# Stick-breaking attention: running sums over a softplus split in a high and a low part

## The chip, the cores and the metric

The kernel runs on one core of one Trainium2 chip. The metric is the device time of one execution in microseconds (us). Three runs of the kernel before took 1545.80, 1546.03 and 1546.11 us, the median is 1546.03 us. One more execution was profiled; its trace is what the rows below are from.

## The reference

One layer of a hybrid decoder, for 256 tokens of width 2048. The normalised input is projected (`h @ w_in`) into three parallel branches of width 1024 and their gates: a gated MLP over chunks of 128 tokens, a complex diagonal state space model (S5) followed by a GLU, and a stick-breaking attention of 8 heads. The branches are projected back, gated, summed, sent through `w_out`, and a squared-ReLU MLP of width 8192 and a last norm follow. All of it is float32.

The change lies in the attention. For each head and block of 128 queries:

```
z = q @ k.T * scale                          # 128 queries x up to 256 keys
log_1m = where(mask, log_sigmoid(-z), 0)     # minus the softplus of z
after  = cumsum(log_1m, reverse) - log_1m    # sum over the keys behind this one
w = where(mask, exp(log_sigmoid(z) + after), 0)
out = w @ v
```

The exclusive reverse running sum `after` is computed as a product with a strictly triangular matrix of minus ones, and, for keys in the other block, a matrix of minus ones.

## The kernel before, in words

**The main stream.** Every large product is cut into *units* of one 512 KB weight tile. For each unit SyncE loads the float32 tile (line 195), ScalarE casts it to fp32r (`hi`, line 214) and VectorE forms the rest `raw - hi` (`lo`, line 215, shown in the trace as L86, the helper through which all VectorE work is issued). TensorE then multiplies three combinations of high and low parts of weight and activation. `begin_unit` (line 260) converts the unit three ahead, so TensorE has two to three units in hand. There are four `hi` and four `lo` buffers: the cast of unit u+4 waits until TensorE is through with the `hi` of unit u. The units stand in a fixed plan (lines 154 to 185): S5 input, q, k, v for heads 0 to 3, then q, k, v for heads 4 to 7, the gated MLP, eight gates and branches, the four gates of the S5 branch (`gate1`), the GLU (`glu`), the rest. A unit is eight products of one weight part and four or eight more; it takes TensorE about 2.7 to 2.8 us.

**The side tasks.** Attention, S5 and the small preparations are Python generators. After every unit `pump` (line 224) goes through the list of tasks and issues steps of them. The order on each engine is the order in which the program is written; only GpSimd's is left to the scheduler. What `pump` issues after unit n stands on TensorE between the units n and n+1, and on ScalarE and VectorE behind the conversion issued with unit n.

**The account of `pump`.** VectorE's calls are metered in planner's nanoseconds, `(180 if n <= 128 else 65) + n * (0.52 if fast else 1.042)` for n elements per partition (line 85; `tensor_scalar` is fast, `tensor_sub` is not). After each unit the credit rises by 2560 and falls by what was metered since, with a cap of 5120; in short:

```
credit[0] = min(credit[0] + UNIT_NS - V.spent, NCRED * UNIT_NS)
V.spent = 0.0
for ent in list(tasks):
    while credit[0] > V.spent:
        c = next(ent[1])          # one step of the task
        if c == BAR: break        # go on with it after the next unit
```

A task that yields `BAR` stops until the next pump; a yielded number is compared with `BAR` and used for nothing else. Attention is put at the front of the list, `s5` at its end. `drain(name)` (line 237) runs a task to its end at once, with no unit between its steps; `do_glu` (line 1069) calls `drain("s5")`, since the GLU needs S5's output `gs`.

**S5's end** (lines 793 to 832): 16 chunks, each ending in a rotation of four VectorE steps (`rotate`); then `BAR`, `BAR`, the product `y_mm(7)` on TensorE (line 772), `BAR`, `y_evac(7)` (one VectorE operation and a Gelu on ScalarE, lines 778 and 780), `BAR`, and four `split2` (line 399), each a cast on ScalarE and a subtraction on VectorE, which give `gs`.

**Attention** (line 838): four pairs of heads. For a pair: scores `pz` (lines 847, 848), `BAR`, scaled copy and mask `za`, `BAR`, Abs, Exp and Ln on ScalarE (lines 861 to 863), `BAR` twice, then two VectorE operations of 768 elements that give the softplus `sp` and, in place, `za` (lines 866, 867), `BAR`, the running sums `pc` (lines 873 to 876), `BAR`, `le = pc + za` and Exp (lines 880 to 882), `BAR`, the product with v, `pyc` (lines 890, 892), `BAR`, the split of the output. The three blocks of `sp` lie side by side in a row of 384 columns: (keys 0, queries 0), (keys 0, queries 1), (keys 1, queries 1). All operands of `pc` are float32. The tiles of activations come from one pool of 32 buffers (`a4`, line 130).

Of the kernel before, what the change touches and what calls it, by code (L numbers as in the profile page):

```python
# [10 lines left out]
F32 = mybir.dt.float32  # L11
F32R = mybir.dt.float32r
I32 = mybir.dt.int32
AF = mybir.ActivationFunctionType
ALU = mybir.AluOpType
AX = mybir.AxisListType

P = 128
D = 2048
T = 256  # L20
# [71 lines left out]
def hybrid_trunk(  # L92
# [22 lines left out]
    V, S, G, PE = Metered(nc.vector), nc.scalar, nc.gpsimd, nc.tensor  # L115
# [14 lines left out]
    def a4(shape, dt, name):  # L130
        return acts.tile(shape, dt, tag="a4", name=name)
# [3 lines left out]
    def cst(shape, name, dt=F32):  # L135
        return const.tile(shape, dt, tag=name, name=name)

    def t2k(shape, name):
        return s5w.tile(shape, F32, tag="t2k", name=name)

    def side(name):
        return ps_sd.tile([P, 512], F32, tag="sd", name=name)
# [250 lines left out]
    def split1(dst, kt, src):  # L393
        S.copy(dst.hi(kt), src)
        V.tensor_sub(dst.lo(kt), src, dst.hi(kt).bitcast(F32))
# [35 lines left out]
    def load_x(c):  # L431
# [19 lines left out]
    ones = cst([P, P], "ones")  # L451
# [1 line left out]
    ident = cst([P, P], "ident")  # L453
    G.affine_select(out=ident, in_=ones, pattern=[[1, P]], compare_op=ALU.is_equal,
                    fill=0.0, base=0, channel_multiplier=-1)
    nones = cst([P, P], "nones")
    G.memset(nones, -1.0)

    ntri = cst([P, P], "ntri")
    G.affine_select(out=ntri, in_=nones, pattern=[[-1, P]], compare_op=ALU.is_gt,  # L460
                    fill=0.0, base=0, channel_multiplier=1)


    pw = side("pwarm")
# [373 lines left out]
    def attention(half):  # L838
        scale = 1.0 / math.sqrt(P)
        fl = "p e b t -> p (e b t)"  # L840
        for hb in (2 * half, 2 * half + 1):
            hs = (2 * hb, 2 * hb + 1)
            pz = []
            for h in hs:
                q, k = qT[h // 4][:, h % 4, :], kT[h // 4][:, h % 4, :]
                p = side(f"pz{h}")
                PE.matmul(p[:, 0:T], lhsT=k[:, 0:P], rhs=q, start=True, stop=True)
                PE.matmul(p[:, T:T + P], lhsT=k[:, P:T], rhs=q[:, P:T], start=True, stop=True)
                pz.append(p)
            yield BAR  # L850
            za = a4([P, 2, 3, P], F32, f"za{hb}")
            le = a4([P, 2, 3, P], F32, f"le{hb}")
            for e in range(2):
                S.activation(za[:, e].rearrange("p b t -> p (b t)"), pz[e][:, 0:T + P], AF.Copy, scale=scale)

                G.affine_select(out=za[:, e, 0:3:2, :], in_=za[:, e, 0:3:2, :], pattern=[[0, 2], [1, P]],
                                compare_op=ALU.is_gt, fill=-1e30, base=0, channel_multiplier=-1)
            yield BAR
            sp = a4([P, 2, 3, P], F32, f"sp{hb}")
            zf, lf, sf = za.rearrange(fl), le.rearrange(fl), sp.rearrange(fl)  # L860
            S.activation(lf, zf, AF.Abs)
            S.activation(lf, lf, AF.Exp, scale=-1.0)
            S.activation(lf, lf, AF.Ln, bias=1.0)
            yield BAR
            yield BAR
            V.scalar_tensor_tensor(out=sf, in0=zf, scalar=0.0, in1=lf, op0=ALU.max, op1=ALU.add)
            V.scalar_tensor_tensor(out=zf, in0=zf, scalar=0.0, in1=lf, op0=ALU.min, op1=ALU.subtract)
            yield 1700
            yield BAR
            pcs = []  # L870
            for e, h in enumerate(hs):
                pc = side(f"pc{h}")
                PE.matmul(pc[:, 0:T], lhsT=ntri, rhs=sp[:, e, 0:2, :].rearrange("p b t -> p (b t)"),
                          start=True, stop=False)
                PE.matmul(pc[:, P:T], lhsT=nones, rhs=sp[:, e, 2, :], start=False, stop=True)
                PE.matmul(pc[:, T:T + P], lhsT=ntri, rhs=sp[:, e, 2, :], start=True, stop=True)
                pcs.append(pc)
            yield BAR
            for e in range(2):
                V.tensor_add(le[:, e].rearrange("p b t -> p (b t)"), pcs[e][:, 0:T + P],  # L880
                             za[:, e].rearrange("p b t -> p (b t)"))
            S.activation(lf, lf, AF.Exp)
            yield 1000
            yield BAR
            v = vN[hb // 2]
            pys = []
            for e, h in enumerate(hs):
                p = side(f"pyc{h}")
                c0 = (h % 4) * P
                PE.matmul(p[:, 0:T], lhsT=v[:, 0, c0:c0 + P],  # L890
                          rhs=le[:, e, 0:2, :].rearrange("p b t -> p (b t)"), start=True, stop=False)
                PE.matmul(p[:, P:T], lhsT=v[:, 1, c0:c0 + P], rhs=le[:, e, 2, :], start=False, stop=True)
                pys.append(p)
            yield BAR
            for e, h in enumerate(hs):
                split1(yc, h, pys[e][:, 0:T])
            yield 700
# [105 lines left out]
    def do_nat(kind, i, us):  # L1003
        dsts = vN if kind == "v" else vg

        def ev(tt, ps):
            if tt == 0:
                dsts[i] = a4([P, NT, 512], F32, f"{kind}{i}")
            dst = dsts[i]
            S.activation(dst[:, tt, :], ps, AF.Gelu_apprx_tanh if kind == "vg" else AF.Copy,  # L1010
                         scale=r1[0][:, tt:tt + 1])
            if kind == "vg":
                sumsq(dst[:, tt, :], ssv[:, tt, i:i + 1], ps)
            if kind == "v" and tt == 1:
                spawn(f"att{i}", attention(i))
            if kind == "vg" and i == 1 and tt == 1:
                spawn("gmlp", gmlp())

        if kind == "vg" and i == 1:
            gmlp_load()  # L1020
        run_N(us, xs, ev)
# [253 lines left out]
```

## Time and profile before

| what | value |
|---|---|
| median of three runs | 1546.03 us |
| profiled execution | 1545.78 us, its span 1544.1 us |
| TensorE busy | 1528.4 us (99%) |
| VectorE busy | 1097.1 us (71%) |
| ScalarE busy | 764.0 us (49%) |
| mean granted TensorE clock | 0.998 |

The span runs from the first to the last instruction of the profiled execution. A line such as `L873 PE MATMUL pc<-sp,ntri` names the line of the kernel, the engine (PE is TensorE, PEld its weight load, DVE VectorE, ACT ScalarE, POOL GpSimd), the operation, and the tiles written and read. A float32 product appears as two pairs of weight load and matmul, an fp32r product as one. The durations of matmuls include their fill and drain, so that neighbours overlap; what a product costs in a stream is the distance of the starts.

### The profile page before, as it was taken

How to read it: one execution, taken by the hardware profiler on the slowest of the kernel's cores; microseconds unless marked ns; L12 is line 12 of the kernel's file. 1: busy time of each engine (PE TensorE's matmuls, PEld its weight loads, DVE VectorE, ACT ScalarE, POOL GpSimd, SP SyncE). 2: the span in 40 equal slices, each digit the busy share in tenths (PEclk: the TensorE clock that was granted, in tenths of full speed). 3: DMA queues.
4: the chain of work that ended last, by engine and by line, in shares of the span. 5: the costliest groups of instructions: out<-in, count | busy, mean ns of one | idle time of the engine just before them, and what ended most of it. 6: DMA issues, size and time to landing. Idle time of an engine off the chain costs nothing.

```text
span 1544.1 us, 20755 instructions
## 1 busy us (share of the span) xinstructions
PE 1528.4 (99%) x7900; PEld 1303.8 (84%) x7900; DVE 1097.1 (71%) x1454; ACT 764.0 (49%) x947; POOL 67.3 (4%) x126
## 2 busy tenths in 40 slices
PE   9999999999999999999999999999999999999997
PEld 9988888888888888898888888888888888888886
DVE  6886988989999999967655665466545564556554
ACT  7546577555546555564444443344434444344442
POOL 0301021001001000000000000000000000000000
PEclk9999999999999999999999999999999999999999
DMA  9965565657666666656666555555555555555653
GB/s 342 328 199 164 186 211 172 197 175 225 202 212 212 199 215 200 192 177 209 205 202 194 188 189 193 196 187 188 192 195 191 188 188 193 195 190 187 219 194 105
DMA packets 97411, 308.67 MB, mean 200 GB/s; under 512 B 11296, under 2 KB 22560, under 8 KB 97312
## 3 DMA queue, kind: packets, MB, share of 16 engines
q1 hardware_dynamic: 79200, 285.25, 56.2%
q0 software_dynamic: 11904, 10.49, 3.2%
q10 hardware_dynamic: 6208, 11.61, 2.4%
q8 instruction: 62, 1.02, 0.3%
q14 instruction: 37, 0.30, 0.1%
HBM read 301.02 MB, written 6.29 MB: 199 GB/s over the span
## 4 chain that ended last, share of the span: by engine, by line
PE 96%; DVE 1%; issue 1%; ACT 1%; DMA 1%; SPq 0%; POOLq 0%; POOL 0%; DVEq 0%; ACTq 0%
PE mm L289 21%; PE mm L351 19%; PE mm L352 19%; PE mm L354 19%; PE mm L293 11%; PE mm L320 1%; PE mm L321 1%; PE mm L328 1%; PE py L772 1%; PE pb L674 0%; DMA raw<-in_w_in 0%; ACT hi L214 0%; DVE lo L86 0%; DMA raw<-in_w_m 0%; DVE x L86 0%
## 5 line engine op out<-in xcount | busy, mean ns | idle before, releaser
L86 DVE TENSOR_TENSOR lo<-raw,hi 128x1024 fp32r<-128x1024 f32 (+1 forms) x537 | 653.3, 1220 | 380.1 <-ACT hi L214 365.5
L214 ACT CAST hi<-raw 128x1024 fp32r<-128x1024 f32 (+1 forms) x537 | 561.4, 1049 | 634.7 <-PE mm L352 397.7
L289 PE MATMUL mm<-xz,hi 128*128 128x512 f32 x1024 | 256.5, 392 | 0.0
L289 PEld LDWEIGHTS mm<-xz,hi 128*128 128x128 f32 x1024 | 184.4, 189 | 33.2
L351 PE MATMUL mm<-hi,xs 128*128 128x512 f32 x512 | 200.8, 392 | 0.0
L352 PE MATMUL mm<-hi,xs 128*128 128x512 f32 x512 | 199.5, 390 | 0.0
L352 PE MATMUL mm<-hi,ff 128*128 128x512 f32 x480 | 186.8, 389 | 0.0
L351 PE MATMUL mm<-hi,ff 128*128 128x512 f32 x480 | 186.8, 389 | 0.0
L293 PEld LDWEIGHTS mm<-xz,lo 128*128 128x128 f32 x1024 | 139.7, 190 | 10.0
L293 PE MATMUL mm<-xz,lo 128*128 128x256 f32 x1024 | 142.8, 282 | 0.0
L354 PE MATMUL mm<-lo,xs 128*128 128x512 f32 x512 | 137.0, 389 | 0.0
L354 PE MATMUL mm<-lo,ff 128*128 128x512 f32 x480 | 128.3, 389 | 0.0
L351 PEld LDWEIGHTS mm<-hi,xs 128*128 128x128 f32 x512 | 96.1, 188 | 21.9 <-ACT bu L681 1.6
L354 PEld LDWEIGHTS mm<-lo,xs 128*128 128x128 f32 x512 | 96.1, 188 | 20.2
L352 PEld LDWEIGHTS mm<-hi,xs 128*128 128x128 f32 x512 | 96.2, 188 | 19.4
L352 PEld LDWEIGHTS mm<-hi,ff 128*128 128x128 f32 x480 | 90.1, 188 | 18.7
L354 PEld LDWEIGHTS mm<-lo,ff 128*128 128x128 f32 x480 | 90.1, 188 | 18.7
L351 PEld LDWEIGHTS mm<-hi,ff 128*128 128x128 f32 x480 | 90.1, 188 | 18.6
L289 PE MATMUL mm<-xs,hi 128*128 128x512 f32 x384 | 96.6, 393 | 0.3 <-DVE s5x L86 0.3
L289 PEld LDWEIGHTS mm<-xs,hi 128*128 128x128 f32 x384 | 69.1, 189 | 13.3 <-ACT hi L214 0.5
L86 DVE TENSOR_TENSOR rt<-bu,cs 128x1024 f32<-128x1024 f32 x64 | 76.8, 1221 | 0.3
L293 PEld LDWEIGHTS mm<-xs,lo 128*128 128x128 f32 x384 | 52.4, 190 | 3.8
(252 smaller groups left out, 1681.3 us busy)
## 6 DMA issues: line engine op xcount, KB each, us to landing
raw<-in_w_m SPq DMA_DIRECT2D x256, 512.0 KB, 4.3
raw<-in_w_in SPq DMA_DIRECT2D x143, 512.0 KB, 4.2
raw<-in_w_wide SPq DMA_DIRECT2D x48, 512.0 KB, 4.4
raw<-in_w_br SPq DMA_DIRECT2D x48, 512.0 KB, 4.3
raw<-in_w_out SPq DMA_DIRECT2D x32, 512.0 KB, 3.8
x<-in_x ACTq DMA_DIRECT2D x8, 512.0 KB, 5.8
raw<-in_w_glu SPq DMA_DIRECT2D x8, 512.0 KB, 4.3
bs<-bd POOLq DMA_DIRECT2D x48, 64.0 KB, 4.7
```

The source lines that it names most:

```text
L86: return fn(*a, **kw)
L214: S.copy(hi[:, k, :], raw[:, k, :])
L289: PE.matmul(pt[:, nb, :], lhsT=hi[:, k, nb * P:(nb + 1) * P], rhs=src.both(4 * i + k), start=4 * i + k == 0, stop=False)
L293: PE.matmul(pt[:, nb, T:], lhsT=lo[:, k, nb * P:(nb + 1) * P], rhs=src.hi(4 * i + k), start=False, stop=4 * i + k == last)
L320: PE.matmul(po, lhsT=wh, rhs=src.hi(kt), start=kt == 0 and nb % 2 == 0, stop=False)
L321: PE.matmul(po, lhsT=wh, rhs=src.lo(kt), start=False, stop=False)
L328: PE.matmul(po, lhsT=lo[:, k, nb * P:(nb + 1) * P], rhs=src.hi(kt), start=False, stop=kt == 2 * nk - 1 and nb % 2 == 1)
L351: PE.matmul(ps[tt], lhsT=xh, rhs=hi[:, k, :], start=kt == 0, stop=False)
L352: PE.matmul(ps[tt], lhsT=xl, rhs=hi[:, k, :], start=False, stop=False)
L354: PE.matmul(ps[tt], lhsT=xh, rhs=lo[:, k, :], start=False, stop=kt == 2 * nk - 1)
L772: PE.matmul(py[h][32 * i:32 * i + 32, :T], lhsT=cks[h][:, ri, i, :], rhs=s[i // 2][:, ri, i % 2, :], start=ri == 0, stop=ri == 1, tile_pos ...
```

## The change

`sp` is split after it is computed: `sh` is its fp32r cast (ScalarE), `sl` the rest (VectorE). The running sums are then fp32r products: for `sh` and for `sl` one of 384 columns with the triangular matrix, over all three blocks at once, and one of 128 columns with the matrix of minus ones. Both constant matrices become fp32r, written by VectorE (`tensor_scalar`) in place of GpSimd; the triangular one is first built by GpSimd in a tile `tri` of the two-buffer pool `t2k`. The number yielded behind the step changes.

```diff
-    nones = cst([P, P], "nones")
-    G.memset(nones, -1.0)
-
-    ntri = cst([P, P], "ntri")
-    G.affine_select(out=ntri, in_=nones, pattern=[[-1, P]], compare_op=ALU.is_gt,
+    nones = cst([P, P], "nones", F32R)
+    V.tensor_scalar(out=nones, in0=ones, scalar1=-1.0, scalar2=None, op0=ALU.mult)
+
+    ntri = cst([P, P], "ntri", F32R)
+    tri = t2k([P, P], "tri")
+    G.affine_select(out=tri, in_=ones, pattern=[[-1, P]], compare_op=ALU.is_gt,
                     fill=0.0, base=0, channel_multiplier=1)
+    V.tensor_scalar(out=ntri, in0=tri, scalar1=-1.0, scalar2=None, op0=ALU.mult)
...
             V.scalar_tensor_tensor(out=zf, in0=zf, scalar=0.0, in1=lf, op0=ALU.min, op1=ALU.subtract)
-            yield 1700
+            sh, sl = (a4([P, 2, 3, P], F32R, f"sp{n}{hb}") for n in "hl")
+            S.copy(sh, sp)
+            V.tensor_sub(sl, sp, sh.bitcast(F32))
+            yield 2600
             yield BAR
             pcs = []
             for e, h in enumerate(hs):
                 pc = side(f"pc{h}")
-                PE.matmul(pc[:, 0:T], lhsT=ntri, rhs=sp[:, e, 0:2, :].rearrange("p b t -> p (b t)"),
-                          start=True, stop=False)
-                PE.matmul(pc[:, P:T], lhsT=nones, rhs=sp[:, e, 2, :], start=False, stop=True)
-                PE.matmul(pc[:, T:T + P], lhsT=ntri, rhs=sp[:, e, 2, :], start=True, stop=True)
+                for n, s in enumerate((sh, sl)):
+                    PE.matmul(pc[:, 0:T + P], lhsT=ntri, rhs=s[:, e].rearrange("p b t -> p (b t)"),
+                              start=n == 0, stop=False)
+                    PE.matmul(pc[:, P:T], lhsT=nones, rhs=s[:, e, 2, :], start=False, stop=n == 1)
                 pcs.append(pc)
```

## Rows read from the trace of the kernel before

**Rows 1.** The page, busy time of each engine and its share of the span.

```profile
PE 1528.4 (99%) x7900; PEld 1303.8 (84%) x7900; DVE 1097.1 (71%) x1454; ACT 764.0 (49%) x947; POOL 67.3 (4%) x126
```

**Rows 2.** Timeline of TensorE around the second pair's sums: start us, duration us, what.

```profile
171.57 2.00 PE L289 MATMUL mm<-xs,hi 128*128 128x512 f32 x8
173.41 1.12 PE L293 MATMUL mm<-xs,lo 128*128 128x256 f32 x8
174.37 0.60 PE L873 MATMUL pc<-sp,ntri 128*128 128x256 f32 x2
...
176.36 0.39 PE L352 MATMUL mm<-hi,xs 128*128 128x512 f32 x1
```

**Rows 3.** Timeline of the opening, GpSimd, TensorE and VectorE.

```profile
1.05 4.84 PE L467 MATMUL pwarm<-ones 128*128 128x128 f32 x24 [1.05 <-POOL ones L452]
...
1.44 0.28 POOL L460 TENSOR_SCALAR_AFFINE_SELECT ntri<-nones 128x128 f32<-128x128 f32 x1
...
4.27 0.89 DVE L86 SCALAR_TENSOR_TENSOR xs<-xf,colv,xs 128x256 fp32r<-128x256 f32 x2 [3.18 <-ACT xs L419]
```

**Rows 4.** Timeline of the first pair's softplus and sums, on three engines.

```profile
128.14 0.84 ACT L861 ACTIVATE le<-za 128x768 f32<-128x768 f32 x1
...
133.20 1.03 ACT L214 CAST hi<-raw 128x1024 fp32r<-128x1024 f32 x1
...
134.27 1.23 DVE L86 TENSOR_TENSOR lo<-raw,hi 128x1024 fp32r<-128x1024 f32 x1 [4.77 <-ACT hi L214]
...
135.09 0.58 ACT L302 COPY wq<-mm 128x512 f32<-128x512 f32 x1
...
137.66 1.28 ACT L732 ACTIVATE td<-cs,s_cs 128x128 f32<-128x128 f32 x4 [1.99 <-DVE cs L86]
...
138.16 1.11 PE L293 MATMUL mm<-xs,lo 128*128 128x256 f32 x8
...
140.00 0.95 DVE L86 SCALAR_TENSOR_TENSOR sp<-za,le 128x768 f32<-128x768 f32 x1
140.99 0.96 DVE L86 SCALAR_TENSOR_TENSOR za<-za,le 128x768 f32<-128x768 f32 x1
...
141.01 0.70 PE L873 MATMUL pc<-sp,ntri 128*128 128x256 f32 x2 [1.73 <-DVE sp L86]
...
142.76 0.55 PEld L674 LDWEIGHTS pb<-su,bs 96*128 96x128 f32 x4
...
143.00 1.13 DVE L86 SCALAR_TENSOR_TENSOR cs<-cs,s_cs,td 128x128 f32<-128x128 f32 x4
```

**Rows 5.** Timeline, the exponential behind the sums, first pair and second pair.

```profile
145.19 1.01 DVE L86 TENSOR_TENSOR le<-pc,za 128x384 f32<-128x384 f32 x2
...
146.28 1.28 ACT L882 ACT_TABLE_LOAD   x1 [5.45 <-DVE le L86]
...
182.50 0.85 ACT L882 ACTIVATE le<-le 128x768 f32<-128x768 f32 x1 [1.97 <-DVE le L86]
```

**Rows 6.** Timeline of S5's end and the first unit of the GLU.

```profile
655.00 1.28 DVE L86 TENSOR_TENSOR bu<-rt,rt 128x512 f32<-128x512 f32 x2
656.21 3.72 DVE L86 TENSOR_TENSOR lo<-raw,hi 128x1024 fp32r<-128x1024 f32 x3
...
661.13 1.07 PE L772 MATMUL py<-bu,ck 128*32 128x256 f32 x16
...
662.56 0.47 DVE L86 SCALAR_TENSOR_TENSOR s5x<-s5x,colv,py 128x256 f32<-128x256 f32 x1
...
664.03 2.50 DVE L86 TENSOR_TENSOR gs<-s5x,gs 128x512 fp32r<-128x512 f32 x4 [0.99 <-ACT gs L400]
...
665.03 0.28 PE L320 MATMUL mm<-gs,hi 128*128 128x256 f32 x1
```

**Rows 7.** Stretches near the end: stretch, us, busy of PE, PEld, DVE, ACT, POOL, PEclk, DMA.

```profile
1532.00:1533.00 1.00, 0.80 (x7) 0.59 (x5) 0.16 (x1) 0.00 (x0) 0.00 (x0) 1.00 0.00 0
...
1537.00:1538.00 1.00, 0.00 (x0) 0.00 (x0) 0.00 (x0) 0.00 (x0) 0.00 (x0) 0.82 1.10 324
```

## The prediction, made before the kernel was run

> **What bounds the kernel now.** I read the page first: TensorE is busy for 1528.4 of 1544.1 us, so 15.7 us are idle, nearly all of it in the opening and behind the last product; VectorE and ScalarE have 71% and 49% [rows 1]. The list of waits then gives TensorE one real wait in the middle, and it is at this very line: 1.73 us for the first pair's softplus [rows 4]. Last I read the timeline at that wait, at a pair that does not wait, and at the place where S5's result is handed to the GLU. TensorE time removed is therefore time won, but only where VectorE and ScalarE still deliver in time; and the side tasks are rationed by pump's account, so VectorE work added anywhere pushes S5's end back.
>
> **The running sums, pairs two to four.** In the second pair two heads' sums begin at 174.37; the second product behind them starts at 176.36, 0.23 after the first, so 1.76 us for two heads, 0.88 for one [rows 2]. An fp32r product of 512 columns costs (173.41 - 171.57) / 8 = 0.23, one of 256 columns (174.37 - 173.41) / 8 = 0.12 [rows 2]; 384 columns lie between, 0.17. An fp32r product of 128 columns has no row. Its ends: half of a 256-column one, 0.06; or as many passes as float32, 512 column steps, 0.22. I take 0.12, the nearest row, since each such product still loads 128 columns of weights. A head then costs 2 x (0.17 + 0.12) = 0.58 and wins 0.30: six heads, **-1.8 us** (ends -2.5 and -0.6). Each of these pairs gains units between softplus and sums, so the added cast and subtraction are covered: followed through the code, pump's account puts the sums 4, 3 and 4 pumps behind the softplus, where it was 2. Without that cover each pair would wait up to 1.8 us.
>
> **Startup.** VectorE now makes both constants. It waits for GpSimd's last select, done at 1.72, and has nothing else from its memsets to 4.27, after 3.18 us idle [rows 3]. Time: none; uncovered, two operations of half the columns of the pair that takes 0.89 there, so 0.5 at most. But the planner charges them 2 x (180 + 128 x 0.52) = 493.
>
> **Pair one.** When v is done (unit 40) the account stands at 191; less 493 it is negative, so attention starts one unit later. Sums still follow the softplus by one pump. A unit of q is 8 x 0.23 + 8 x 0.12 = 2.8 [rows 2]; unit 45 ends at 138.16 + 1.11 = 139.27, unit 46 at 142.07. ScalarE's Abs, Exp and Ln take 128.14 to 133.20, 5.1 us [rows 4]; one unit later they run from 130.9 to 136.0, and the next hi (1.03) is there at 137.05. VectorE, idle for it, then has the same work ahead of the softplus as it had from 134.27 to 140.00: two lo, the q evacuation, an S5 table, 5.73 us [rows 4]. The softplus starts at 142.8 and is done (0.95) at 143.7. The cast `sh` lies between a copy of 512 columns, 0.58, and a cast of 1024, 1.03 [rows 4]: 0.82, done at 144.6. `za` ends at 144.65; the subtraction, at `sp`'s 0.95, at 145.55. TensorE stands still from 142.07 to 144.65, does one head's high part, waits for `sl`, and has 0.29 + 0.58 left: done at 146.45. From the unit's end that is 4.4 us; before it was 142.76 - 139.27 = 3.5 [rows 4]. **+0.9 us** (ends: no wait left, -2.3; one more lo of 1.22 ahead of the softplus, +2.1).
>
> **What is late next.** ScalarE now does the S5 copies `td` (1.28) behind `sh`, so the next hi is there at 146.9; VectorE waits for it, does that lo, the table (1.13) and another lo [rows 4], and reaches `le` at 150.5, done at 151.5 [rows 5]. Exp needs 0.85, and 1.28 more if the table is loaded only after the wait, as in pair one; in pair two it did not come between [rows 5]. It is ready at 152.3 or 153.6; TensorE asks for it after the S5 product (0.55) and two units, at 152.6. Wait 0 or 1.0: **+0.5 us**. The main stream behind does not wait: it is three units ahead.
>
> **S5's end.** The planner is charged 4 x (65 + 768 x 1.042) = 3461 for the four subtractions, with startup 3954. Until here the account's highest value is 4475 of 5120, so none of it is forgiven. Attention goes first; S5 pays. A unit with no other VectorE work leaves 2560 - (65 + 1024 x 1.042) = 1428, so S5 comes 2.8 units later. Does it have them? The last rotation ends, three units' lo follow with no task between, `y_mm(7)` stands at 661.13, one unit comes behind it, and the GLU starts at 665.03 [rows 6]. Call that last unit L. Before, the rotation ends in the pump of L-4 (account 916, charged 1197), the two BARs take L-3 and L-2, `y_mm` comes in L-1, `y_evac` in L, the splits in the drain. At L-2 the account would be 2575, less 3954 it is -1379, more than the last two steps (1197): not done. At L-1 it is 4003 - 3954 = 49: just done. L takes the second BAR, and the drain issues `y_mm`, `y_evac` and splits with no unit between. TensorE then waits out the chain that the last unit hid: VectorE's 0.47 at once, Gelu, cast, first subtraction (a quarter of 2.50): 662.56 to 664.03 + 0.63, 2.1 us [rows 6]. **+2.1 us** (ends: 0, if `y_mm` still stands ahead of L; 3.3, if a lo of 1.2 sits before it on VectorE).
>
> **The rest.** The yielded 2600 is read by nobody. ScalarE gains 4 x 0.82, VectorE 4 x 0.95; behind them wait the next hi and lo, which are three units early. Eight more tiles in the pool of 32: no row shows a wait that they would add; between 0 and 1 us, I take 0. SP's queue is not touched, GpSimd loses a memset.
>
> **Sum:** -1.8 + 0.9 + 0.5 + 2.1 = +1.7. The profiled execution took 1545.78, its span 1544.1; it lies 0.25 below the median of 1546.03, so 1547.5 there and **1547.7** against the median. A measurement of this kernel can tell about 0.2%, 3.1 us, from no change: this is inside.
>
> **The rivals.**
> (a) *TensorE-bound throughout*, both waits absent: -1.8 - 2.3 = -4.1, 1541.9. For it: 99% busy. Against it: both places have no unit to spare by the code's own order. 0.05.
> (b) *S5 still in time*, if the account is other than I follow: +1.7 - 2.1 = -0.4, 1545.6. The margin of 49 only decides how late, not whether. 0.10.
> (c) *Cheap narrow products*, at 0.06: -2.5 + 0.7 + 0.5 + 2.1 = +0.8, 1546.8. For it: half the columns of a 256 one; against it: the weights are no fewer. The Trainium skill ("TensorE: Matmul & The Clock Gate", Back-to-back issue gap) puts a pair of load and 128-column product at about 81 ns, which would be an estimate of +1.1; no row here shows it. 0.12.
> (d) *Narrow products are as slow as float32*, in `pc`'s products with `nones`, 0.22 each: -0.6 + 1.2 + 0.5 + 2.1 = +3.2, 1549.2, **slower**. It decides from 0.21 on. For it: no fp32r product under 256 columns is in the trace; against it: nothing in the rows shows cost rising as columns fall. 0.12.
> (e) *The clock falls* in pair one's wait of 2.6 us. The rows: full clock through the 1.73 us wait; behind the last product (1532.8) it fell only within 1537 to 1538 [rows 7]. Price: the opening's 24 products took 4.84 us, 0.20 each where full clock needs 0.11 (a 256-column pass is as long), 2.2 us [rows 2, 3]: +3.9, 1549.9. The Trainium skill ("TensorE: Matmul & The Clock Gate", HAM oscillation) warns that gaps between bursts make the next products start at half clock, which speaks against the change; the rows so far do not. 0.05.
> (f) *Pair one or the pool costs a conversion more*: +1.2 to +2, 1549.3. 0.08.
> My forecast keeps 0.48.
>
> **The numbers.** Range 1544.7 (b with cheap narrow products) to 1550.0 (d or f with the longer ends); outside are (a) and combinations of (d) to (f). Faster by over 0.2%: (a), 0.05. Slower: half of (d), (e), half of (f), and 0.05 from the forecast's upper end, 0.21. Within: 0.74.
>
> **What would show it.** The head's pitch in pairs two to four near 0.58. In pair one a TensorE wait of 2 to 3 us before `pc`, a shorter one between high and low part. `y_mm(7)` directly ahead of the first GLU product, with about 2 us idle between, and no such idle before. Clock 1.00 in both. VectorE's busy time up by about 4 us, ScalarE's by 3. I am wrong if the GLU starts without a wait, if TensorE's busy time falls by clearly more than 3 us, or if a wait appears in pairs two to four.

## The result, and the profile after

The changed kernel took 1555.99 us (median of four runs, 1554.84 to 1557.1) against 1545.91 of the kernel before: ratio 1.0065, 95% interval 1.0053 to 1.0077, so 10 us **slower**, far outside the range of 1544.7 to 1550.0. The profiled execution has a span of 1553.1 us, 9.1 more than before.

The page first, the line of busy time:

```profile
PE 1531.7 (99%) x7884; PEld 1306.5 (84%) x7884; DVE 1102.7 (71%) x1460; ACT 767.6 (49%) x952; POOL 71.4 (5%) x125
```

VectorE gained 5.6 us and ScalarE 3.6. Of that the added instructions are 4.3 (four subtractions of 0.95 and two constants of 0.23) and 3.3 (four casts of 0.84). But TensorE, with 16 products fewer in the record and 2 us of work removed, is busy 3.3 us *longer* than in [rows 1]: the same work was done more slowly somewhere. The list of waits says where to look (waits in all, times, longest, us):

```profile
PE mm L289 <- DVE s5x L86: 3.1, 1, 3.1
PE pc L879 <- ACT sph L871: 2.6, 1, 2.6
PE mm L320 <- ACT gs L400: 1.9, 1, 1.9
...
PE py L774 <- DVE le L86: 0.8, 1, 0.8
PE pc L879 <- DVE spl L86: 0.4, 1, 0.4
PE mm L321 <- DVE gs L86: 0.3, 1, 0.3
```

The waits for `sph`, `gs` and `spl` were forecast. That of `py` was not, nor was the first, the longest: it is nowhere near the attention. The table goes through the stream, part by part. It takes the start of each unit's first product from the timeline and gives how much time TensorE lost between two units against the trace before (us; a plus is time lost). Unit 16 is the first of q, 41 to 52 hold pair one, 225 is the GLU's second.

| part | changed | changed, again | charges alone | nothing charged | + one step | before + one step | + two steps apart |
|---|---|---|---|---|---|---|---|
| opening, to 15 | -0.89 | -0.25 | -0.62 | -0.30 | -0.26 | -0.40 | -0.96 |
| S5's input, 15 to 40 | +2.79 | +3.81 | +2.58 | +0.35 | +0.03 | +0.04 | +0.77 |
| pair one, 40 to 52 | +3.74 | +2.54 | +0.02 | +2.54 | -1.66 | -1.98 | -2.24 |
| pairs two to four, 52 to 140 | -0.91 | -0.87 | +0.09 | -0.89 | -1.08 | +0.09 | -1.84 |
| S5's end, 140 to 225 | +4.33 | +2.98 | +2.98 | -0.01 | 0.00 | -0.01 | 0.00 |
| in all | +9.06 | +8.21 | +5.05 | +1.69 | -2.97 | -2.26 | -4.27 |

The columns behind the first are the experiments below: "+ one step" is "nothing charged" with one scheduling step (one `BAR`) more, "+ two steps apart" with two at different places. Behind unit 225 nothing moves any more.

**S5's input.** The unit that waits needs a PSUM buffer that VectorE must first empty (`s5x`). Timeline of the changed kernel there: first ScalarE, then VectorE, then TensorE.

```profile
48.78 1.05 ACT L214 CAST hi<-raw 128x1024 fp32r<-128x1024 f32 x1 [3.73 <-DMA raw<-in_w_wide]
```

```profile
49.86 1.23 DVE L86 TENSOR_TENSOR lo<-raw,hi 128x1024 fp32r<-128x1024 f32 x1 [1.75 <-ACT hi L214]
51.01 1.22 DVE L86 TENSOR_TENSOR bl<-br,bh 128x1024 fp32r<-128x1024 f32 x1
...
53.83 1.23 DVE L86 TENSOR_TENSOR lo<-raw,hi 128x1024 fp32r<-128x1024 f32 x1
54.97 1.28 DVE L86 TENSOR_TENSOR s5x<-mm,rbc 128x512 f32<-128x512 f32 x2
```

```profile
56.40 2.08 PE L289 MATMUL mm<-xs,hi 128*128 128x512 f32 x8 [3.12 <-DVE s5x L86]
```

And the same stretch of VectorE before:

```profile
48.23 1.22 DVE L86 TENSOR_TENSOR bl<-br,bh 128x1024 fp32r<-128x1024 f32 x1
49.37 1.22 DVE L86 TENSOR_TENSOR lo<-raw,hi 128x1024 fp32r<-128x1024 f32 x1
...
51.95 1.23 DVE L86 TENSOR_TENSOR lo<-raw,hi 128x1024 fp32r<-128x1024 f32 x1
53.09 1.28 DVE L86 TENSOR_TENSOR s5x<-mm,rbc 128x512 f32<-128x512 f32 x2
```

`bl` is the second half of the split of S5's B, a side task (lines 524, 525). It stood one `lo` earlier; now it stands behind the `lo` of 49.86, which waits for a cast, which waits for a weight load. VectorE idles for 1.75 us and then has the split still to do, ahead of the evacuation TensorE waits for, which begins at 54.97 where it was 53.09.

**Pair one.** The timeline of TensorE, and under it stretches of 1 us (us, busy of PE, PEld, DVE, ACT, POOL, PEclk, DMA):

```profile
142.85 1.11 PE L293 MATMUL mm<-xs,lo 128*128 128x256 f32 x8
146.58 0.54 PE L879 MATMUL pc<-sph,ntri 128*128 128x384 f32 x1 [2.61 <-ACT sph L871]
...
147.57 0.69 PE L879 MATMUL pc<-spl,ntri 128*128 128x384 f32 x1 [0.35 <-DVE spl L86]
...
150.19 3.58 PE L289 MATMUL mm<-xs,hi 128*128 128x512 f32 x8
153.60 1.12 PE L293 MATMUL mm<-xs,lo 128*128 128x256 f32 x8
```

```profile
145.00:146.00 1.00, 0.00 (x0) 0.00 (x0) 0.97 (x2) 0.31 (x1) 0.00 (x0) 1.00 0.42 61
146.00:147.00 1.00, 0.42 (x2) 0.34 (x2) 1.00 (x2) 1.00 (x3) 0.00 (x0) 0.89 0.83 303
147.00:148.00 1.00, 0.65 (x3) 0.43 (x2) 0.52 (x1) 1.00 (x4) 0.00 (x0) 0.50 0.77 287
...
153.00:154.00 1.00, 1.00 (x6) 0.81 (x6) 0.01 (x1) 0.91 (x1) 0.87 (x2) 0.70 0.93 186
```

The two waits, 2.61 and 0.35, are those that were forecast. What follows was not: the granted clock is 0.50, the lower level of 1.2 GHz, from 146.8 to 153.6 (worked out from the stretches at both ends, 0.89 and 0.70). The same eight products of 512 columns that took 173.41 - 171.57 = 1.84 us in [rows 2] take 153.60 - 150.19 = 3.41. This is the work that was done more slowly.

**Pairs two to four**, the second pair's sums on TensorE:

```profile
188.19 0.33 PE L879 MATMUL pc<-sph,ntri 128*128 128x384 f32 x1
188.36 0.22 PE L881 MATMUL pc<-sph,nones 128*128 128x128 f32 x1
188.42 0.39 PE L879 MATMUL pc<-spl,ntri 128*128 128x384 f32 x1
...
189.28 0.45 PE L351 MATMUL mm<-hi,xs 128*128 128x512 f32 x1
```

Two heads take 1.09 us, 1.76 before [rows 2]: 0.67 for a pair, 2.0 for three.

**S5's end**, VectorE and TensorE, and the clock behind it:

```profile
668.21 1.28 DVE L86 TENSOR_TENSOR bu<-rt,rt 128x512 f32<-128x512 f32 x2
668.58 1.59 PE L774 MATMUL py<-bu,ck 128*32 128x256 f32 x16
...
672.03 0.39 PE L320 MATMUL mm<-gs,hi 128*128 128x256 f32 x1 [1.86 <-ACT gs L400]
672.75 0.58 PE L321 MATMUL mm<-gs,hi 128*128 128x256 f32 x1 [0.34 <-DVE gs L86]
```

```profile
672.00:673.00 1.00, 0.63 (x2) 0.43 (x3) 0.99 (x2) 1.00 (x3) 0.00 (x0) 0.72 0.86 324
673.00:674.00 1.00, 1.00 (x6) 1.00 (x7) 1.00 (x3) 1.00 (x3) 0.00 (x0) 0.50 0.25 98
```

`y_mm(7)` now stands directly ahead of the GLU, with no unit between [rows 6], and half clock follows here too, until 675.8.

### The profile page after: what moved, and what is told of

The parts are those of the page before. It is cut to its first block, busy times and chain, and to the rows that moved or that the text cites. A ratio compares the mean times of both kernels' runs of the same rounds, so it can differ in the third digit from the quotient of the medians.

```text
span 1553.1 us, 20740 instructions
## 1 busy us (share of the span) xinstructions
PE 1531.7 (99%) x7884; PEld 1306.5 (84%) x7884; DVE 1102.7 (71%) x1460; ACT 767.6 (49%) x952; POOL 71.4 (5%) x125
## 4 chain that ended last, share of the span: by engine, by line
PE 92%; DVE 2%; issue 1%; ACT 1%; DMA 0%; POOLq 0%; POOL 0%; DVEq 0%; ACTq 0%
PE mm L289 20%; PE mm L351 19%; PE mm L352 19%; PE mm L354 19%; PE mm L293 10%; DVE lo L86 1%; PE mm L321 1%; PE mm L320 1%; PE mm L328 0%; PE pb L676 0%; PE py L774 0%; ACT hi L214 0%; DVE bu L86 0%; DMA raw<-in_w_m 0%; DVE x L86 0%
```

## The experiments

The theory: the work that was added is not what costs; **the numbers that `pump`'s account charges for it** move S5's steps to worse places, at its input and at its end, and in pair one the longer chain of softplus, cast and subtraction makes TensorE wait until its clock falls. The rivals: the added VectorE and ScalarE time itself; the constants; the clock as a matter apart. An operation issued with `nc.vector` in place of `V` is the same instruction, but is not metered. "Charged" below means metered in this account.

**The constants uncharged.**

```diff
-    V.tensor_scalar(out=nones, in0=ones, scalar1=-1.0, scalar2=None, op0=ALU.mult)
+    nc.vector.tensor_scalar(out=nones, in0=ones, scalar1=-1.0, scalar2=None, op0=ALU.mult)
...
-    V.tensor_scalar(out=ntri, in0=tri, scalar1=-1.0, scalar2=None, op0=ALU.mult)
+    nc.vector.tensor_scalar(out=ntri, in0=tri, scalar1=-1.0, scalar2=None, op0=ALU.mult)
```

> The changed kernel, the two constants written by VectorE as before but not metered in pump's account. Account theory (the losses come from what pump is charged, since it moves steps to other units): the 3.1 us wait of TensorE ahead of the first q unit falls back to about 0.4, the rest stays (pair one waits some 3 us with the clock at half behind it, the GLU waits 2 us with the clock at half); about 2.5 us faster than the changed kernel, 1553.5. Work theory (the losses come from the added cast and subtraction themselves, whoever is charged for them): as the changed kernel, 1556.

Measured: 1558.92 us, ratio 1.0083 (1.0068 to 1.0098), a miss. The wait at S5's input is gone (0.5), but two new ones came among the later pairs, with half clock behind each (from 235.3 and from 272.8); the timeline of TensorE there:

```profile
234.97 1.67 PE L774 MATMUL py<-bu,ck 128*32 128x256 f32 x16 [4.15 <-ACT bu L683]
...
272.35 0.77 PE L895 MATMUL pyc<-le,v 128*128 128x256 f32 x2 [1.80 <-ACT le L887]
```

What follows: without the charge of 493 the wait at S5's input is not there. (How long it is with the charge varies; see "the changed kernel again".) Where the account stands otherwise also decides on which other engine's work a step of S5 falls; why it fell so badly here was not followed up.

**The subtraction uncharged.**

```diff
-            V.tensor_sub(sl, sp, sh.bitcast(F32))
+            nc.vector.tensor_sub(sl, sp, sh.bitcast(F32))
```

> The changed kernel, the four subtractions done but not metered. Account theory: S5 ends in time, y_mm(7) stands one unit ahead of the GLU again, no wait there and full clock: 4.4 us faster than the changed kernel, 1551.6; the wait ahead of the first q unit stays. Work theory: the GLU still waits, 1556.

Measured: 1548.33, ratio 1.0022 (1.0012 to 1.0033). This is faster than expected. S5's end costs nothing: no wait is listed at the GLU. So it is the 3461 of the four subtractions that make that wait. S5's input still waits, 1.6.

**Nothing charged**: both edits.

> The changed kernel, constants and subtractions done but neither metered, so that pump's order is that of the kernel before. Account theory: only pair one's waits are left (2.5 to 3 us for the cast, then 0.5 to 1 for the subtraction, half clock behind), pairs two to four win 2.0: about 1549. Work theory: 1556.

Measured: 1547.93, ratio 1.0012 (1.0003 to 1.0022). All the work is there, and of the 9.06 us only 1.69 are left. TensorE's waits:

```profile
PE pc L879 <- ACT sph L871: 2.6, 1, 2.6
...
PE mm L289 <- DVE s5x L86: 0.7, 1, 0.7
```

**The charges alone**: the kernel before, with the charges and without the work.

```diff
+    V.spent += 2 * (180 + 128 * 0.52)
...
             V.scalar_tensor_tensor(out=zf, in0=zf, scalar=0.0, in1=lf, op0=ALU.min, op1=ALU.subtract)
+            V.spent += 65 + 768 * 1.042
             yield 1700
```

> The kernel before, with none of the change's instructions, but with pump's account charged as in the change: 493 at the start and 865 in each pair. Account theory: the waits ahead of the first q unit (about 3 us) and ahead of the GLU (about 2 us, and half clock behind) appear without any added work: 5 to 7 us slower than before, about 1552. Work theory: as before, 1546.

Measured: 1551.61, ratio 1.0039 (1.0026 to 1.0052), as expected; but the half clock that was expected behind the GLU's wait did not come in the profiled execution. Numbers in the planner, with no instruction behind them, cost 5.05 us of span:

```profile
PE mm L289 <- DVE s5x L86: 2.9, 1, 2.9
PE mm L320 <- ACT gs L400: 1.9, 1, 1.9
PE pc L876 <- DVE sp L86: 1.7, 1, 1.7
```

Two of the changed kernel's three long waits, and pair one's wait is the 1.7 of before [rows 4]. With the run before, this shows from both sides that the account is the cause of the waits at S5's input and at its end. That of pair one is not the account's.

**Nothing charged, one step more** between the split and the sums.

```diff
             yield 2600
             yield BAR
+            yield BAR
             pcs = []
```

> e3 (nothing charged) with one more BAR between the softplus split and the running sums, so that the sums stand one unit later. Account theory with latency: pair one's wait for the cast goes, at most 0.6 us for the subtraction is left, the clock stays at 1.00; with pairs two to four's win of 2.0 less some 1 us of waits for PSUM that e3 showed, 3 to 4 us faster than before: 1542.5. Work theory (VectorE and ScalarE cannot carry the split): no faster than before, 1546 or more.

Measured: 1543.07, ratio 0.998 (0.9971 to 0.9989): faster than both kernels, clock 1.00 from the opening to the last product. Here pair one's sums start at the unit's end, so the wait of 2.6 came from the chain of softplus, cast and subtraction, which was too long for the room it had.

```profile
PE pyc L896 <- ACT le L888: 0.8, 2, 0.5
PE mm L320 <- ACT hi L214: 0.5, 1, 0.5
PE mm L289 <- DVE s5x L86: 0.4, 1, 0.4
```

**Two steps more** at that place.

> e3 with two more BARs at the same place. Latency theory: no wait in pair one at all, 0.3 to 0.6 us faster than e5, 1542; if it is not faster than e5, the wait for the subtraction was already gone with one BAR.

Measured: 1546.71, ratio 1.0003 (0.9995 to 1.0012), a miss. The sums are now so late that the product with v waits in a later pair, and half clock follows once more:

```profile
274.28 0.70 PE L897 MATMUL pyc<-le,v 128*128 128x256 f32 x2 [2.80 <-ACT le L889]
```

**Pair one kept busy**: nothing charged, and eight products of float32 that nothing reads, while TensorE waits.

```diff
+            if hb == 0:
+                pd = side("pd")
+                for _ in range(8):
+                    PE.matmul(pd[:, 0:P], lhsT=ones, rhs=ones, start=True, stop=True)
```

> e3 with eight float32 products of 128 columns on constants (some 1.7 us of TensorE) written between the last unit and pair one's sums, so that TensorE is busy in most of the wait; their result is read by nobody. If idle time is what drops the clock: 1.00 throughout and 1 to 1.7 us faster than e3 (half of its 3.4 us at half clock, less what the products delay), 1546.5. If the clock is set otherwise: the half-clock stretch stays and the time is that of e3, 1548, or more.

Measured: 1547.35, ratio 1.0008 (0.9999 to 1.0017), not separable from 'nothing charged'. The clock stayed at 1.00 in the profiled execution; of the kernel's ten executions six have a mean granted clock of 0.998, of the ten with nothing charged none (0.995 to 0.997). By unit 47 pair one costs 1.0 us (2.5 with the fall), by unit 52 1.8, and by unit 140 the two kernels have lost the same since unit 40 (1.66 and 1.65). A stretch of the clock, and the second of two waits that are listed here and not with nothing charged:

```profile
142.00:143.00 1.00, 0.50 (x2) 0.30 (x2) 1.00 (x2) 1.00 (x4) 0.00 (x0) 1.00 0.42 116
```

```profile
186.94 0.70 PE L899 MATMUL pyc<-le,v 128*128 128x256 f32 x2 [0.77 <-ACT le L891]
```

The product with v waits for the exponential, 0.5 us in pair one and 0.8 in pair two. So in these two executions the time won at full clock was waited away again: the fall's 1.7 us (half of 3.4 us at half clock) are paid in pair one and given back by pair two, as the fall slows TensorE where it would have waited. (The added tile also takes one of the four PSUM buffers of the side tasks; what that does was not separated.)

**The GLU kept busy**: the changed kernel, with the same eight products behind `y_mm(7)`.

> The changed kernel with eight such products between y_mm(7) and the GLU's first product. If idle time drops the clock: 1.00 at the GLU and about 1.5 us faster than the changed kernel, 1554.5, the wait itself (2.2 us) staying. Otherwise 1556 or more.

Measured: 1550.84, ratio 1.0035 (1.0021 to 1.0048), less than expected. S5's end costs 2.98 with the clock at 1.00, in place of 4.33: the fall is worth 1.35 there. That the added products held the clock is not shown: in the second execution of the changed kernel, below, and with the charges alone it stayed at 1.00 behind the same wait without them. The rest came from elsewhere: in this execution S5's input waited 0.7, with the order of the changed kernel. That left open what sets the size of that wait.

**The changed kernel again**, unaltered.

> The changed kernel again, unaltered, for the spread of unit 16's wait, which in runs with the same order of the work there was 3.1, 2.9, 1.6 and 0.7 us. If the lateness of a weight load (w_wide, which the cast ahead of the split of S5's B waits for) sets its size: the wait is about 3 us where that cast starts at 48.8 us or later, 1.6 at about 47.7 and 0.7 at 47.2 or earlier, and pair one's wait stays 2.6 + 0.4. If the order alone sets it: 3 us whenever the second half of B is split ahead of it. Time 1551 to 1557 us by the first, 1555 to 1557 by the second.

Measured: 1554.64, ratio 1.0058 (1.0044 to 1.0072). The five executions with this order at S5's input:

| execution | ScalarE's cast begins | VectorE's idle time ahead of `lo` and `bl` | `s5x` begins (before: 53.09) | wait |
|---|---|---|---|---|
| GLU kept busy | 47.18 | 0.16 | 53.14 | 0.7 |
| subtraction uncharged | 47.66 | 0.38 + 0.61 | 54.29 | 1.6 |
| changed | 48.78 | 1.75 | 54.97 | 3.1 |
| charges alone | 48.90 | 2.21 | 55.05 | 2.9 |
| changed, again | 49.10 | 2.00 | 55.12 | 2.6 |

The evacuation is late by VectorE's idle time, and that by the cast, which in the last four stands behind a load (in the second, also that of B). So the order makes the wait possible and a late load sets its size; before, the split filled the time of such a load. With nothing charged, in the old order, that cast began at 48.05, later than in the second row, and VectorE did not idle: `s5x` began at 53.12. (The wait is also shorter by as much as TensorE arrives later from the opening.) Why the load lands at 47 in one execution and at 49 in another stays open. In this execution the clock fell behind S5's input (stretches as above) and in pair one, but not at the GLU:

```profile
57.00:58.00 1.00, 1.00 (x6) 0.75 (x4) 1.00 (x2) 0.00 (x0) 0.00 (x0) 0.75 0.91 271
58.00:59.00 1.00, 1.00 (x4) 0.80 (x3) 0.73 (x2) 0.00 (x0) 0.00 (x0) 0.50 1.12 341
...
672.00:673.00 1.00, 0.39 (x1) 0.19 (x1) 0.49 (x1) 1.00 (x3) 0.00 (x0) 1.00 0.89 229
```

**The kernel before, one step more**: how much of 1543.07 is the step.

> The kernel before with one more scheduling step between softplus and the running sums and nothing else: how much of the 1543.07 us of 'nothing charged, one step more' is the step, and how much the change. If the step is worth what the waits say (1.73 us of standing still in pair one goes, and nothing else moves): 1544.2 us, and the change itself is then worth 1.1 us (2.0 saved in pairs two to four, less what the longer chain leaves). If the step is worth nothing without the change: 1545.9, and the whole 2.9 us are the change's. If the later sums are late for what waits behind them, as with two steps more: 1546 to 1548, with waits of the first products on the coefficients in pairs two to four.

Measured: 1543.67, ratio 0.9986 (0.9977 to 0.9995). The step alone wins 2.2 us, with the old sums and no wait in attention at all. The change's own share is 0.6 us, which the two intervals do not separate from nothing; by the starts of units it is 2.97 - 2.26 = 0.7. Pairs two to four win 1.08 + 0.09 = 1.2 of the 2.0 they save in products; 0.7 of the 0.8 between is lost at pair two's product with v, where TensorE waits for the exponential (the longer of the two waits listed with "one step more").

**The blocks apart**: one step more, the split kept, the third block in a product of its own.

```diff
-                    PE.matmul(pc[:, 0:T + P], lhsT=ntri, rhs=s[:, e].rearrange("p b t -> p (b t)"),
+                    PE.matmul(pc[:, 0:T], lhsT=ntri, rhs=s[:, e, 0:2, :].rearrange("p b t -> p (b t)"),
                               start=n == 0, stop=False)
                     PE.matmul(pc[:, P:T], lhsT=nones, rhs=s[:, e, 2, :], start=False, stop=n == 1)
+                for n, s in enumerate((sh, sl)):
+                    PE.matmul(pc[:, T:T + P], lhsT=ntri, rhs=s[:, e, 2, :], start=n == 0, stop=n == 1)
```

> The kernel of 'nothing charged, one step more' (1543.07 us) with the split in high and low part kept, but the third block in a product of its own: for each part one product of 256 columns and two of 128, in place of one of 384 and one of 128. It prices the second half of the change by itself. If a product of 128 columns behind another costs 0.06 us (half of a 256-column one, as the trace of the change suggests: the next product started 0.06 behind it), 256 + 128 + 128 costs 0.12 + 0.06 + 0.06 = 0.24 and the merged pair 0.285, so laying the blocks side by side saves nothing: head pitch 0.48 to 0.57, time 1543. If the 128-column product costs 0.12, as I took it before: head pitch 0.72, eight heads 1.1 us more, 1544.

Measured: 1543.23, ratio 0.9983 (0.9974 to 0.9992): the same time. The pitch does differ, the second pair's two heads:

```profile
180.36 0.28 PE L880 MATMUL pc<-sph,ntri 128*128 128x256 f32 x1
180.47 0.22 PE L882 MATMUL pc<-sph,nones 128*128 128x128 f32 x1
180.53 0.34 PE L880 MATMUL pc<-spl,ntri 128*128 128x256 f32 x1
180.70 0.22 PE L882 MATMUL pc<-spl,nones 128*128 128x128 f32 x1
180.76 0.27 PE L884 MATMUL pc<-sph,ntri 128*128 128x128 f32 x1
180.88 0.27 PE L884 MATMUL pc<-spl,ntri 128*128 128x128 f32 x1
...
181.67 0.45 PE L351 MATMUL mm<-hi,xs 128*128 128x512 f32 x1
```

1.31 us, 0.65 a head, between my two expectations. Of the 0.88 before, the two fp32r parts in place of the float32 products save 0.23 and the blocks side by side 0.11 (1.09 / 2 = 0.545).

**One step more before the product with v** as well.

```diff
             S.activation(lf, lf, AF.Exp)
             yield 1000
             yield BAR
+            yield BAR
```

> 'Nothing charged, one step more' with one scheduling step more between the exponential and the product with v too. If the two remaining waits of that product for the exponential (0.5 and 0.3 us) are lateness by less than a unit, they go and nothing takes their place: 1542.3 us. If each pair's chain as a whole is late, the wait moves to a later step of the pair or to the next pair, as with two steps more ahead of the sums: 1543 to 1546.

Measured: 1541.7, ratio 0.9972 (0.9961 to 0.9983), 4.0 us faster than before and the fastest kernel of the study. No wait of attention is left, and pairs two to four now keep 1.84 of their 2.0. The kernel before with both steps was not run, so how much of this last 1.4 is the change's is open.

## Why the prediction was wrong

**Pairs two to four: the products right, their cover not.** Forecast -1.8, measured -2.0 in products. The head's pitch was 0.545 for 0.58: rival (c)'s narrow product is what a product of 128 columns behind a wider one showed, 188.42 - 188.36 = 0.06, and rival (d)'s 0.22 fell. But the cover was not whole: of the 2.0, 0.91 was left at unit 140; the one wait listed there is that of a product of S5 for `le`, 0.8. That was named as a sign of being wrong ("if a wait appears in pairs two to four").

**Startup: the step that failed.** "Time: none; [...] But the planner charges them 2 x (180 + 128 x 0.52) = 493." The time was right and the charge was right, but the charge was followed only to pair one and to S5's end. The account is one number for all tasks: it first reached S5's preparation, while S5's input was still being multiplied, and moved steps of its coefficients and the split of B by one unit. Measured: +2.8 and +3.8 us in two executions, in the part that had no term.

**Pair one: the wait right, the clock not.** Forecast 2.6 us and then a wait for `sl`; measured 2.61 and 0.35 to 0.5. Rival (e), the fall of the clock, had 0.05, and its price of 2.2 us; it came in every profiled execution with this wait (six of six), and the part cost +2.5 to +3.7 in place of +0.9 and +0.5. Without the fall the two terms were of the right size: with pair one kept busy they came out at 1.0 and 0.8. With it, the wait for the exponential, forecast at 0.5, did not come. Rows 7 had misled: there the clock fell some 5 us behind the last product, and I took that for how long it holds. The Trainium skill ("TensorE: Matmul & The Clock Gate", HAM oscillation) says that waits between bursts of products bring the half clock back. Its example has longer waits than this one of 2.61; the trace agrees on the fall, with 0.50 from 146.8 to 153.6.

**S5's end: the mechanism right, the term too small.** `y_mm` in the drain, no unit behind it, 2.1 us forecast. The wait for the first quarter of `gs` is 1.86; two more were not counted: `y_mm` itself, issued so soon that it waits inside for the second rotation (1.59 for 1.07), and the GLU's second product, which waits for the subtraction (672.75 - 672.03 = 0.72 for 0.12). 1.86 + 0.52 + 0.60 = 2.98, as measured without a fall. In the profiled execution the clock adds 1.35.

**The sum**, for the profiled execution: 2.8 at S5's input that was not there, 2.3 too little in pair one, 2.2 at S5's end, 0.9 in pairs two to four, less 0.9 of an opening that ran ahead. That is 7.4 on top of +1.7: the 9.1 of the table.

**The range and the chances** failed with the steps. The range had no end for S5's input, and held the clock as one small chance at one place, where the same cause could act at each wait. The parts given for "slower" add up to 0.20, not 0.21.

## What to carry to other kernels

Where an order of work is made by a meter, an edit is also a change of the meter's readings: list every task that draws on it and follow the charge to each, or issue the new work unmetered and compare. A wait of TensorE of 2 to 3 us can bring half clock behind it, so it is not to be priced by its length alone; how much of that stays depends on whether TensorE would have waited behind it anyway. And before crediting a change with what its best version wins, give the old kernel the same room: here one scheduling step was worth 2.2 us, the change behind it some 0.6, which the runs do not separate from nothing.

## What the hardware showed that was not expected

The clock does not follow the length of the wait alone. It fell behind each of six waits of 2.6 us in pair one, behind 2.8 (two steps more), behind 4.15 and 1.80 (constants uncharged), and behind one of 2.6 at S5's input; it did not fall behind 3.1 (the changed kernel) and 2.9 (charges alone) at S5's input. At the GLU the same wait of 1.86 was followed by half clock in one execution and by 1.00 in two others. Between the opening and the last product, all but one of the stretches at half clock lasted 3.4 us, that one 6.8. Nor does the fall come at once: in the changed kernel's second execution pair one's products began again at 148.24 and the clock fell near 149.7. Keeping TensorE busy with products that nothing reads held it at 1.00 in pair one, where it had fallen in six executions of six. At the GLU that is not shown, since the clock also stayed up there without them.
